# Two-block network in float32 on one core: block 2 heads transposed into other PSUM tiles, VectorE's order set for key rounds and boundary sums, a third relu buffer, the delta solve one step later

## The chip, the cores and the metric

The kernel runs on one core of one Trainium2 chip, as one launch. The metric is the time of that launch on the device in microseconds (us). Of the kernel before, three runs took 2660.15, 2661.12 and 2662.5 us; the median is 2661.12 us.

## The reference

A sequence of 512 tokens of width 1024 goes through two blocks of two layers each. Every layer is a mixer and a feed-forward part (FFN), each with an RMS norm before it, one behind it, and a residual sum. Cut to what matters:

```python
def first_block(x, ...):                      # 2 layers
    h = rms_norm(x, norm_pre_mix[l])
    proj = h @ w_in[l]                        # dilated attention, 8 heads of 64, and
    attn = dilated_attention(aq, ak, av)      # a gated delta rule, 4 heads of 128,
    o = gated_delta_rule(dq, dk, dv, beta, g) # which inverts (I + A) by chunks
    mix = concat([attn, rms_norm(o) * silu(z)]) @ w_out[l]
    x = x + rms_norm(mix, norm_post_mix[l])
    x = x + rms_norm(conv_glu_ffn(rms_norm(x, ...)), norm_post_ffn[l])

def second_block(x, ...):                     # 2 layers
    u_pool, q, k, v, iq, ik, iw = split(rms_norm_2(x, g_pre_mix[l]) @ w_in[l])
    score = einsum('bqh,bqhs->bqs', iw, relu(iq . ik))   # indexer, 8 heads of 64
    keep the 128 best of the allowed keys of each query  # top_k
    b_out = softmax attention of q over the kept keys, 8 heads of 64
    mix = concat([pool_mixer(u_pool), b_out]) @ w_out[l]
    x = x + rms_norm_2(mix, g_post_mix[l])
    x = x + rms_norm_2(square(relu(h @ w_ff1[l])) @ w_ff2[l], g_post_ffn[l])
```

## The kernel before

Everything stays in SBUF but the weights, which stream in. Each product of matrices is done as three matmuls (L234 to L236) of high and low parts, since one pass has not the precision wanted. So each 512 KB piece of weights is loaded by SyncE's (SP's) DMA queue into one of two `wr` buffers (L186), rounded by ScalarE (ACT) into `wh` (L212), and the rest is put into `wl` by VectorE (DVE), for some pieces of block 2 by GpSimd (POOL) (L214).

TensorE's (PE's) results go to PSUM in three sets of banks: `mm` (four, the large products), `ax` (two) and `dx` (two).

The order of the work is that in which the program is written out and a scheduler then lays it down, engine by engine. Each engine works its own row in order. The program is a set of generators: `weave` advances a main one (a product of matrices) and with each of its steps the side ones in `fill` by one step each, so that a `yield` is what moves work between places. Where nothing says otherwise, the scheduler sets an instruction into its engine's row where its own estimate of times makes it ready.

Three places bear on the change.

**Block 2, the indexer** (L1499). For each block `i` of 128 queries, `score(i)` takes eight heads' products with the keys (PE L660, two at a time, in both `ax` banks), lets ACT take the relu of each into an `rl` buffer (L1534; two buffers), copies the first with a weight to `sc` (L1536), and has VectorE add the other seven (L1538). `select(i)` then finds the 128 best keys of `sc` in 16 rounds on VectorE, each a MAX8 (L1551) and a MATCH_REPLACE8 (L1552) over 128(i+1) columns: 256, 384 and 512 for i of 1, 2 and 3. A mask `nm` comes of it (L1555), which the attention reads (L693) and the first block of queries doesn't need. `select(1)` runs beside `score(2)`, `select(2)` beside `score(3)`, and `select(3)` beside the attention. In the same stretch `heads_split` (L663) turns the heads of q and k: four PE transposes (L620) into an `ax` bank, two ACT copies (L667, L761) and a VectorE subtract (L762). Layer 1 of block 2 repeats layer 0 some 614 us later.

**The boundary** (L565), at the end of every mixer and FFN but the last: the sum of squares of the product goes through `rsqrt` on VectorE (L443 to L457, tiny instructions), PE copies the result across partitions (`replicate`, L472), VectorE and ACT update x (L561, L562, L481, L482), and `stats_sum` (L485) adds up the squares of the new x for the next norm, on VectorE and on POOL (L493).

**The delta rule's solve** (`delta_chain`, L964). It gathers small triangles through two scratch tensors in DRAM: SP writes `scx` and `scw` (L1061) and reads them back, spread over 128 partitions, into `dqv` and `dW` (L1062). Four yields later the first PE matmul on `dqv` is written (L1078); `dW` is first read at L1091.

Of the kernel before, what the change touches and what calls it, by code (L numbers as in the profile page):

```python
# [9 lines left out]
F32 = mybir.dt.float32  # L10
# [3 lines left out]
OP = mybir.AluOpType  # L14
AX = mybir.AxisListType

P = 128
S = 512
# [73 lines left out]
class Net:  # L92
# [345 lines left out]
    def rsqrt(self, v, n, out=None, factor=None):  # L438

        V, sm = self.nc.vector, self.sm  # L440
        new = lambda name: sm.tile([P, 16], F32, name=name)[:, :n]
        i = sm.tile([P, 16], I32, name="rqi")[:, :n]
        V.tensor_scalar(i, v.bitcast(I32), 1, None, op0=OP.logical_shift_right)  # L443
        V.tensor_scalar(i, i, -1, RSQ, op0=OP.mult, op1=OP.add)
        y, h, t, u, z = i.bitcast(F32), new("rqh"), new("rqt"), new("rqu"), new("rqz")
        V.tensor_tensor(t, y, y, op=OP.mult)
        V.tensor_scalar(h, v, 64.0 / 9.0, None, op0=OP.mult)
        V.tensor_tensor(t, t, v, op=OP.mult)
        V.tensor_scalar(z, y, -0.375 * RSQ_A, None, op0=OP.mult)
        V.scalar_tensor_tensor(z, t, -RSQ_B, z, op0=OP.add, op1=OP.mult)  # L450
        V.tensor_tensor(t, z, z, op=OP.mult)
        V.tensor_tensor(t, t, h, op=OP.mult)
        V.scalar_tensor_tensor(u, t, -10.0 / 3.0, t, op0=OP.add, op1=OP.mult)
        if factor is not None:
            V.tensor_tensor(z, z, factor, op=OP.mult)
        y = out if out is not None else new("rqy")
        V.scalar_tensor_tensor(y, u, 5.0, z, op0=OP.add, op1=OP.mult)  # L457
        return y

    def col_sums(self, parts, pt):  # L460
# [104 lines left out]
    def boundary(self, B, steps_a, steps_b, lead, gap):  # L565


        gname, l, need_rep, tok = B["nxt"]
        for st in steps_a:
            st()  # L570
            yield
        self.place_next(2, B["pool"], B["wnext"])
        self.prefetch(4)
        for st in steps_b[:lead]:
            st()
            yield
        ra = self.post_rms(B, 0)
        for st in steps_b[lead:lead + gap]:
            st()
            yield  # L580
        rep_a = self.replicate(ra, 2)
        for k in range(NK):
            self.post_update(B, 0, k, rep_a)
        for st in steps_b[lead + gap:]:
            st()
            yield
        rb = self.post_rms(B, 1)
        pts = [self.mm() for _ in range(4)]
        gen = (self.gemm_tok_halves if tok else self.gemm_feat_halves)(pts, self.xs, 8)
        for i in range(2):  # L590
            next(gen)
            yield
        rep_b = self.replicate(rb, 2)
        for k in range(NK):
            self.post_update(B, 1, k, rep_b)
        for n, todo in ((3, lambda: self.stats_sum(0, B["gt"], need_rep)), (5, lambda: self.stats_sum(1, B["gt"], need_rep)),
                        (2, lambda: self.stats_rms(B["gt"])), (2, lambda: None)):
            for i in range(n):
                next(gen)
                yield  # L600
            todo()
        if need_rep:
            self.stats_rep()
        self.first = pts, gen
# [8 lines left out]
        return dict(gt=gt, mixg=[t[:, k] for t in gt for k in range(4)], pool=pool, parts=[])  # L613


    def transposed(self, src):

        pt = self.ax()
        for pr in range(4):
            self.nc.tensor.transpose(pt[:, pr * P:(pr + 1) * P], src[:, pr * P:(pr + 1) * P], self.ident)  # L620
        return pt.rearrange("p (a b) -> p a b", a=4)
# [41 lines left out]
    def heads_split(self, hl, src, t):  # L663


        p, s = self.transposed(src), slice(t * P, (t + 1) * P)
        self.nc.scalar.activation(self.four(src), p, AF.Copy)  # L667
        self.split_out(self.four(src), hl[0][:, :, s], hl[1][:, :, s])

# [294 lines left out]
    def delta_chain(self, pool, D, l, conv):  # L964
# [67 lines left out]
        p = self.dx()  # L1032
# [27 lines left out]
        for src, scr, dst in ((qt, self.scx, X), (qr, self.scw, W)):  # L1060
            nc.sync.dma_start(self.blocks(scr), src)  # L1061
            nc.sync.dma_start(dst.rearrange("p h t c -> p (h t) c"), self.full(scr))  # L1062
        yield
        yield
        yield
        yield

        for lev in (32, 64, 128):
            half, nb = lev // 2, P // lev
# [372 lines left out]
    def mixer2(self, l):  # L1442
        nc, V, T, tc = self.nc, self.nc.vector, self.nc.tensor, self.tc
        with tc.tile_pool(name=f"m2{l}", bufs=1, reuse_waits="tile") as pool:
            wpool = pool.tile([P, 4, P], F32, name="wpool")
            nc.gpsimd.dma_start(wpool, self.a["w_pool_2"][l].rearrange("g c d -> c g d"))
            xs = self.xs
            pts = yield from self.take_first()
            rcol, rrep = self.rcol, self.rrep
            rq = pool.tile([P, NT], F32, name="rq")  # L1450
            V.tensor_scalar(rq, rcol, -0.125, None, op0=OP.mult)
            ri = pool.tile([P, NT], F32, name="ri")
            V.tensor_scalar(ri, rcol, 0.125, None, op0=OP.mult)
            rw = pool.tile([P, NT], F32, name="rw")
            V.tensor_scalar(rw, rcol, 8.0 ** -0.5, None, op0=OP.mult)
            iA = [pool.tile([P, 4, S], F32R, name=n) for n in ("iqT", "ta")]
            hd = self.heads2(pool, pts, ri, lambda x, t: self.heads_split(iA, x, t), 0)
            pt = self.mm()
            yield from self.gemm_small(pt, xs, 72)
            ikw = pool.tile([72, S], F32, name="ikw")  # L1460
            nc.scalar.activation(ikw, pt[:72], AF.Copy)
            nm = [self.c("nchunk")] + [pool.tile([P, (i + 1) * P], F32, name=f"nm{i}") for i in range(1, NT)]
            D, bufs = {}, []
            fill = [hd, self.indexer(pool, D, iA, ikw, rcol, rw, nm)]
            kk = [pool.tile([P, 4, S], F32R, name=n) for n in ("kT", "w3")]
            qq = [pool.tile([P, 4, S], F32R, name=n) for n in ("qT", "w2")]
            v = pool.tile([P, NT, S], F32, name="v")

            def buf(n):
                if not bufs:  # L1470
                    bufs.extend(pool.tile([P, NT, S], F32, name=b) for b in ("qs", "ta"))
                return bufs[n % 2][:, n // 2 % 4]

            self.on_pool.update(range(self.n_get + 2, self.n_get + 14))
            scores = self.split_scores(qq, lambda pr: [t[:, pr] for t in kk])
            att = self.attention(pool, scores, v, lambda i: nm[i], 4, self.dx, 2, buf, lambda: "mix" in D,
                                 lambda i: "scored" in D and D.get("selected", 0) >= i)
            for name in ("k", "q", "v"):
                pts = [self.mm() for _ in range(4)]
                if name == "v":  # L1480
                    fill.append(self.early(att, 6, 1, lambda: "scored" in D))
                yield from self.weave(self.gemm_tok(pts, xs, NK), fill)
                if name == "k":
                    fill.insert(0, self.heads2(pool, pts, rcol, lambda x, t: self.heads_split(kk, x, t), 2))
                elif name == "q":
                    fill.insert(0, self.heads2(pool, pts, rq, lambda x, t: self.heads_split(qq, x, t), 2))
            for t in range(NT):
                nc.scalar.activation(v[:, t, :], pts[t], AF.Copy, scale=rcol[:, t:t + 1])
            mix = self.xs
            fill.append(self.pool_mix(pool, D, rrep, l, wpool, mix))  # L1490
            yield from self.weave(att, fill)
            while fill:
                yield from self.weave(iter([0]), fill)
            yield from self.out_gemm(pool, mix, None, "g_post_mix_2", l, ("iqT", "qT"), ("kT", "v", "w2", "w3", "w4"),
                                     ("qs", "ta"),
                                     lambda n: pool.tile([P, S], F32, name="sc" if n % 2 else "rl", bufs=2),
                                     ("g_pre_ffn_2", l, False, False))

    def indexer(self, pool, D, iA, ikw, rcol, rw, nm):  # L1499
# [25 lines left out]
        def score(i):  # L1525
            w = (i + 1) * P
            sc = pool.tile([P, S], F32, name="sc", bufs=2)
            for h in range(8):
# [1 line left out]
                    ss = [self.ax() for _ in range(2)]  # L1530
                    scores(ss, i, h // 2)
                p = ss[h % 2]
                rl = pool.tile([P, S], F32, name="rl", bufs=2)
                nc.scalar.activation(rl[:, :w], p[:, :w], AF.Relu)  # L1534
                if h == 0:
                    nc.scalar.activation(sc[:, :w], rl[:, :w], AF.Copy, scale=iw[:, i, 0:1])  # L1536
                else:
                    V.scalar_tensor_tensor(sc[:, :w], rl[:, :w], iw[:, i, h:h + 1], sc[:, :w], op0=OP.mult, op1=OP.add)  # L1538
                if h % 2:
                    yield  # L1540
            V.memset(sc[0:64, w - 64:w], -FMAX)
# [4 lines left out]
        def select(i):  # L1546
            w = (i + 1) * P
            sc = scs[i]
            for it in range(16):
                m8 = self.sm.tile([P, 8], F32, name="m8")  # L1550
                V.max(m8, sc[:, :w])  # L1551
                V.match_replace(sc[:, :w], m8, sc[:, :w], MARK)  # L1552
                if (it % 2, 1, it % 4)[i - 1]:
                    yield
# [126 lines left out]
```

## Time and profile before

| | us |
|---|---|
| median of three runs | 2661.12 |
| the profiled execution | 2660.98 |
| span of its trace | 2659.2 |
| PE busy | 2607.6 |
| VectorE busy | 1559.9 |
| ACT busy | 1125.8 |
| POOL busy | 261.3 |

1.8 us of the profiled execution lie outside the trace's span. The share of busy time tells which engine the rest has to keep fed; what a place costs is read from the idle time of that engine in front of an instruction, and from what released it. The clock that PE was granted stands beside it: in a row of a stretch, 1.00 is 2.4 GHz for all of it and 0.50 would be 1.2 GHz for all of it.

### The profile page before, as it was taken

The page shows a single profiled execution, that of the slowest core. Times are in us where ns is not written, and L with a number is a line of the kernel's source. Part 1 is how long each engine was busy: PE and PEld are TensorE (multiplying, and loading weights), DVE is VectorE, ACT ScalarE, POOL GpSimd, SP SyncE. Part 2 cuts the span into 40 slices and gives each one's busy share as a digit, 9 for nine tenths or more (in the row PEclk, how much of TensorE's full clock was granted, in tenths as well). Part 3 has the DMA queues.
Part 4 walks back from the last instruction along what each step waited for, and adds up shares of the span by engine and source line. Part 5 has one row for each costly group of instructions (what it writes and reads, how often), then busy time and mean ns, then how long its engine had stood idle before and what let it go on. Part 6 is the DMA issues. An engine that isn't in the chain of part 4 may idle for free.

```text
span 2659.2 us, 35443 instructions
## 1 busy us (share of the span) xinstructions
PE 2607.6 (98%) x13656; PEld 2111.8 (79%) x13656; DVE 1559.9 (59%) x3122; ACT 1125.8 (42%) x1916; POOL 261.3 (10%) x356
## 2 busy tenths in 40 slices
PE   8999999999999999999999999999999999999998
PEld 7877788888888869888888667888888766988887
DVE  6946676663586576666636875634326785633434
ACT  5346543342443474433424455324224446423322
POOL 2100100000220002000002431000002330100000
PEclk9999999999999999999999999999999999999999
DMA  5321213333324102233332212133333222133232
GB/s 159 94 83 52 80 41 95 96 95 96 95 82 108 48 33 80 87 95 93 95 107 72 72 56 80 49 95 95 95 96 96 63 61 68 57 95 93 90 95 95
DMA packets 155568, 221.83 MB, mean 83 GB/s; under 512 B 25759, under 2 KB 92039, under 8 KB 155399
## 3 DMA queue, kind: packets, MB, share of 16 engines
q1 hardware_dynamic: 154007, 216.92, 27.1%
q0 software_dynamic: 832, 2.63, 0.3%
q8 instruction: 107, 1.75, 0.3%
q14 instruction: 62, 0.51, 0.1%
q10 hardware_dynamic: 560, 0.01, 0.0%
HBM read 212.70 MB, written 6.83 MB: 83 GB/s over the span
## 4 chain that ended last, share of the span: by engine, by line
PE 82%; DVE 13%; ACT 2%; DMA 1%; POOL 1%; issue 1%; SPq 0%; DVEq 0%; ACTq 0%; POOLq 0%
PE mm L234 20%; PE mm L236 20%; PE mm L235 20%; PE dx L236 2%; PE dx L235 2%; PE dx L234 2%; DVE sc L1552 2%; PE ax L236 2%; PE ax L235 2%; PE ax L234 2%; DVE m L1551 2%; PE ax L730 2%; PE mm L711 1%; DVE hl L482 1%; DVE x L562 1%
## 5 line engine op out<-in xcount | busy, mean ns | idle before, releaser
L236 PE MATMUL mm<-hh,wl 128*128 128x512 f32 (+2 forms) x1924 | 738.5, 384 | 0.0
L234 PE MATMUL mm<-hh,wh 128*128 128x512 f32 (+2 forms) x1924 | 737.1, 385 | 1.4 <-ACT wh L212 1.1
L235 PE MATMUL mm<-hl,wh 128*128 128x512 f32 (+2 forms) x1924 | 737.2, 383 | 0.0
L214 DVE TENSOR_TENSOR wl<-wr,wh 128x1024 fp32r<-128x1024 f32 (+1 forms) x312 | 385.6, 1236 | 590.1 <-ACT wh L212 577.1
L212 ACT ACTIVATE wh<-wr 128x1024 fp32r<-128x1024 f32 (+1 forms) x336 | 354.4, 1055 | 729.2 <-PE mm L235 387.2
L234 PEld LDWEIGHTS mm<-hh,wh 128*128 128x128 f32 (+1 forms) x1924 | 362.7, 189 | 78.6 <-ACT wh L212 1.5
L235 PEld LDWEIGHTS mm<-hl,wh 128*128 128x128 f32 (+1 forms) x1924 | 361.9, 188 | 77.4 <-issue 0.7
L236 PEld LDWEIGHTS mm<-hh,wl 128*128 128x128 f32 (+1 forms) x1924 | 361.0, 188 | 74.8
L234 PE MATMUL mm<-wh,hh 128*128 128x512 f32 x524 | 215.8, 412 | 0.0
L235 PE MATMUL mm<-wl,hh 128*128 128x512 f32 x524 | 210.5, 402 | 0.0
L236 PE MATMUL mm<-wh,hl 128*128 128x512 f32 x524 | 209.6, 400 | 0.0
L234 PEld LDWEIGHTS mm<-wh,hh 128*128 128x128 f32 x524 | 99.6, 190 | 28.0 <-issue 3.7
L236 PEld LDWEIGHTS mm<-wh,hl 128*128 128x128 f32 x524 | 99.8, 191 | 23.7
L235 PEld LDWEIGHTS mm<-wl,hh 128*128 128x128 f32 x524 | 100.0, 191 | 22.7 <-issue 1.8
L1265 DVE TENSOR_TENSOR hl<-hq,hh 128x512 fp32r<-128x512 f32 x92 | 63.0, 687 | 73.0 <-ACT hh L1264 72.9
L1378 ACT ACTIVATE fy<-fxc,par 128x512 f32<-128x512 f32 x88 | 67.1, 810 | 78.5 <-DVE fxc L1375 78.5
L1264 ACT ACTIVATE hh<-hq 128x512 fp32r<-128x512 f32 x92 | 57.2, 622 | 94.7 <-PE dx L235 78.8
L481 ACT ACTIVATE hh<-x,par 128x256 fp32r<-128x256 f32 x128 | 60.4, 503 | 78.1 <-DVE x L562 77.8
L1375 DVE TENSOR_TENSOR fxc<-mm,rrep 128x512 f32<-128x512 f32 x88 | 59.9, 688 | 29.8 <-PE mm L236 25.5
L730 PEld LDWEIGHTS ax<-tb,v 128*64 128x64 f32 x640 | 42.8, 136 | 40.0 <-DVE tb L715 11.5
L730 PE MATMUL ax<-tb,v 128*64 128x128 f32 x640 | 68.9, 286 | 4.8 <-DVE tb L715 4.8
L214 POOL TENSOR_TENSOR wl<-wr,wh 128x1024 fp32r<-128x1024 f32 x24 | 57.5, 2394 | 126.8 <-ACT wh L212 126.8
(666 smaller groups left out, 4468.4 us busy)
## 6 DMA issues: line engine op xcount, KB each, us to landing
wr<-in_w_ff_dram SPq DMA_DIRECT2D x128, 512.0 KB, 3.6
wr<-in_w_in_dram SPq DMA_DIRECT2D x96, 512.0 KB, 3.7
wr<-in_ffn_w_in_dram SPq DMA_DIRECT2D x176, 256.0 KB, 3.2
wr<-in_ffn_w_out_dram SPq DMA_DIRECT2D x44, 512.0 KB, 3.5
wr<-in_w_out_dram SPq DMA_DIRECT2D x32, 512.0 KB, 3.6
xt<-in_x_dram SPq DMA_DIRECT2D x4, 512.0 KB, 7.5
scm<-dM SPq DMA_DIRECT2D x2, 1024.0 KB, 4.5
out_dram<-hq SPq DMA_DIRECT2D x8, 256.0 KB, 2.0
```

The source lines that it names most:

```text
L212: nc.scalar.activation(h[:, :n], r[:, :n], AF.Copy)
L214: eng.tensor_tensor(lo[:, :n], r[:, :n], h[:, :n].bitcast(F32), op=OP.subtract)
L234: t.matmul(out, ah, bh, start=first, stop=False, skip_group_check=shared)
L235: t.matmul(out, ah, bl, start=False, stop=False, skip_group_check=shared)
L236: t.matmul(out, al, bh, start=False, stop=last, skip_group_check=shared)
L481: nc.scalar.activation(self.hh[k][:, c], self.x[k][:, c], AF.Copy, scale=g)
L730: T.matmul(o[self.head_rows(e), h // 2 * P:(h // 2 + 1) * P], v[:, j, (h + e) * 64:(h + e + 1) * 64], pT[e][:, j * P:(j + 1) * P], start=j ...
L1264: nc.scalar.activation(h, hid[k], AF.Copy)
L1265: V.tensor_tensor(lo, hid[k], h.bitcast(F32), op=OP.subtract)
L1375: V.tensor_tensor(xc[:, 2:], pt, rrep, op=OP.mult)
L1378: nc.scalar.activation(y, xc[:, 2:], AF.Identity, scale=w(2), bias=self.pcol("ffn_conv_b", l, r))
L1551: V.max(m8, sc[:, :w])
```

## The change

It makes five edits. The squares' first sum at a boundary (VectorE's L493 of the first half) has to stand behind the last instruction of the second half's `rsqrt`. `heads_split` takes a `dx` bank in place of an `ax` bank (96 transposes and their 24 copies in block 2). The delta solve waits five yields in place of four behind its reads. The `rl` buffers are three in place of two. And each MAX8 of a selection has to stand behind the newest add of the scores that has been written out so far. No engine's instructions change in number; POOL's row is the same as before.

```diff
-        V.scalar_tensor_tensor(y, u, 5.0, z, op0=OP.add, op1=OP.mult)
+        self.rsqrt_end = V.scalar_tensor_tensor(y, u, 5.0, z, op0=OP.add, op1=OP.mult).ins
@@ boundary
+        rb_end = self.rsqrt_end
+        def sum_a():
+            with self.tc.issue_after(rb_end):
+                self.stats_sum(0, B["gt"], need_rep)
-        for n, todo in ((3, lambda: self.stats_sum(0, B["gt"], need_rep)), (5, ...
+        for n, todo in ((3, sum_a), (5, lambda: self.stats_sum(1, B["gt"], need_rep)),
@@ heads_split
-        p, s = self.transposed(src), slice(t * P, (t + 1) * P)
+        p, s = self.transposed(src, self.dx()), slice(t * P, (t + 1) * P)
@@ delta_chain
-        yield
-        yield
-        yield
-        yield
+        for _ in range(5):
+            yield
@@ score
-                rl = pool.tile([P, S], F32, name="rl", bufs=2)
+                rl = pool.tile([P, S], F32, name="rl", bufs=3)
-                    V.scalar_tensor_tensor(sc[:, :w], rl[:, :w], iw[:, i, h:h + 1], sc[:, :w], op0=OP.mult, op1=OP.add)
+                    D["added"] = V.scalar_tensor_tensor(sc[:, :w], rl[:, :w], iw[:, i, h:h + 1], sc[:, :w],
+                                                        op0=OP.mult, op1=OP.add).ins
@@ select
-                V.max(m8, sc[:, :w])
+                with self.tc.issue_after(D["added"]):
+                    V.max(m8, sc[:, :w])
```

Line numbers of the changed kernel are 5 to 7 higher behind the boundary: L1538, L1551, L1552 and L762 become L1543, L1558, L1559 and L768; L1061, L1062 and L1078 become L1067, L1068 and L1084.

VectorE's row in block 2, layer 0, where `select(2)` meets `score(3)`: the rounds are MAX and MATCH_REPLACE of 384 columns (m_13312 belongs to the second round, m_13717 to the last), the adds are 128x512. Before, from the fourteenth round on:

```order
L1551 MAX m_13649<-sc 128x8
L1552 MATCH_REPLACE sc<-m_13649,sc 128x384
L1538 SCALAR_TENSOR_TENSOR sc<-rl,iw,sc 128x512
L1551 MAX m_13676<-sc 128x8
L1552 MATCH_REPLACE sc<-m_13676,sc 128x384
L1551 MAX m_13717<-sc 128x8
L1552 MATCH_REPLACE sc<-m_13717,sc 128x384
L1538 SCALAR_TENSOR_TENSOR sc<-rl,iw,sc 128x512
L1555 TENSOR_SCALAR nm_12738<-sc 128x384
```

and now, from the first round on:

```order
L1559 MATCH_REPLACE sc<-m_13282,sc 128x384
L1562 TENSOR_SCALAR nm_12737<-sc 128x256
L1543 SCALAR_TENSOR_TENSOR sc<-rl,iw,sc 128x512
L1558 MAX m_13312<-sc 128x8
L1559 MATCH_REPLACE sc<-m_13312,sc 128x384
L1543 SCALAR_TENSOR_TENSOR sc<-rl,iw,sc 128x512 x2
L1558 MAX m_13361<-sc 128x8
L1559 MATCH_REPLACE sc<-m_13361,sc 128x384
L768 TENSOR_TENSOR w_12743<-qs,qT 128x4x128 x2
L1543 SCALAR_TENSOR_TENSOR sc<-rl,iw,sc 128x512 x2
```

The first add stood behind the fourteenth round and stands behind the first one now; the last two adds now stand ahead of the fifth round, so that twelve of the sixteen rounds of `select(2)` come behind them. Those twelve and the sixteen of `select(3)` are now mixed with the attention's instructions, and `nm_12739`, the mask of the last block, which stood ahead of the last use of `nm_12737`, now stands right in front of its own first use.

VectorE's row at the boundary behind layer 0's mixer of block 1, before:

```order
L448 TENSOR_TENSOR rqt<-rqt,hv 128x2
L493 TENSOR_TENSOR dqk<-dqk,dqq 128x4x256
L450 SCALAR_TENSOR_TENSOR rqz<-rqt,rqz 128x2
L451 TENSOR_TENSOR rqt<-rqz 128x2
L452 TENSOR_TENSOR rqt<-rqt,rqh 128x2
L453 SCALAR_TENSOR_TENSOR rqu<-rqt 128x2
L457 SCALAR_TENSOR_TENSOR rqy<-rqu,rqz 128x2
```

and now:

```order
L448 TENSOR_TENSOR rqt<-rqt,hv 128x2
L450 SCALAR_TENSOR_TENSOR rqz<-rqt,rqz 128x2
L451 TENSOR_TENSOR rqt<-rqz 128x2
L452 TENSOR_TENSOR rqt<-rqt,rqh 128x2
L453 SCALAR_TENSOR_TENSOR rqu<-rqt 128x2
L457 SCALAR_TENSOR_TENSOR rqy<-rqu,rqz 128x2
L493 TENSOR_TENSOR dqk<-dqk,dqq 128x4x256
```

The sum of squares went from the middle of the `rsqrt` to behind it. On PE the four L472 that take `rqy` also stand some nine 256-column matmuls earlier than before.

SP's row in layer 0 of block 1, where the solve's triangles go out and come back, before:

```order
L1061 DMA scx<-vn 128x16x16
L1061 DMA scw<-dS 128x16x16
L186 DMA wr<-in_w_in_dram 128x2x512
L1062 DMA dqv<-scx 128x16x128
L1062 DMA dW<-scw 128x16x128
L186 DMA wr<-in_w_in_dram 128x2x512 x4
```

and now:

```order
L1067 DMA scx<-vn 128x16x16
L1067 DMA scw<-dS 128x16x16
L1068 DMA dqv<-scx 128x16x128
L186 DMA wr<-in_w_in_dram 128x2x512 x2
L1068 DMA dW<-scw 128x16x128
L186 DMA wr<-in_w_in_dram 128x2x512 x3
```

One load of weights that stood ahead of the read of `dqv` stands behind it, and a second one stands between the reads of `dqv` and `dW`. On PE the first L1078 stands four 512-column matmuls and a group of transposes earlier, and the matmuls between it and the first L1091 have grown from nine to nineteen.

## Rows read from the trace of the kernel before

**Rows 1.** The page: busy us by engine, share of the span, instructions.

```profile
PE 2607.6 (98%) x13656; PEld 2111.8 (79%) x13656; DVE 1559.9 (59%) x3122; ACT 1125.8 (42%) x1916; POOL 261.3 (10%) x356
```

**Rows 2.** Waits of PE over the span: waited for, us in total, times, longest.

```profile
PE ax L620 <- ACT rl L1534: 9.4, 4, 4.2
PE dx L1078 <- DMA dqv<-scx: 5.4, 2, 2.9
...
PE ax L472 <- DVE rqy L457: 4.6, 6, 0.9
...
PE ax L472 <- DVE rcol L457: 1.5, 3, 1.0
```

**Rows 3.** Block 2, layer 0, by stretch: length, busy by engine, PEclk, DMA share, GB/s.

```profile
1528.00:1536.00 8.00, 8.00 (x25) 5.75 (x26) 5.77 (x11) 3.29 (x7) 0.00 (x0) 0.57 0.01 2
...
1543.00:1583.00 40.00, 38.58 (x190) 27.00 (x189) 36.27 (x104) 21.35 (x55) 13.39 (x14) 1.00 0.22 67
1583.00:1600.00 17.00, 16.18 (x99) 9.16 (x97) 11.19 (x38) 13.29 (x35) 4.51 (x6) 1.00 0.10 32
```

**Rows 4.** Timeline, block 2, layer 0: start, us, engine line op [idle before <-releaser].

```profile
1509.42 0.54 DVE L1552 MATCH_REPLACE8 sc<-m,sc 128x384 f32<-128x384 f32 x1
...
1512.87 0.56 DVE L1551 MAX8 m<-sc 128x8 f32<-128x384 f32 x1
...
1514.12 0.56 DVE L1551 MAX8 m<-sc 128x8 f32<-128x384 f32 x1
...
1517.50 0.73 ACT L1536 ACTIVATE sc<-rl,iw 128x512 f32<-128x512 f32 x1
...
1522.51 0.39 PE L234 MATMUL mm<-wh,hh 128*128 128x512 f32 x1
1522.74 0.39 PE L235 MATMUL mm<-wl,hh 128*128 128x512 f32 x1
...
1526.51 0.74 DVE L1538 SCALAR_TENSOR_TENSOR sc<-rl,iw,sc 128x512 f32<-128x512 f32 x1
...
1527.35 0.60 ACT L1534 ACTIVATE rl<-ax 128x512 f32<-128x512 f32 x1 [6.24 <-DVE sc L1538]
...
1528.00 0.66 PE L620 MATMUL ax<-cst,qs 128*128 128x128 f32 x4 [4.19 <-ACT rl L1534]
...
1542.43 0.69 DVE L1551 MAX8 m<-sc 128x8 f32<-128x512 f32 x1
...
1543.95 0.69 DVE L1551 MAX8 m<-sc 128x8 f32<-128x512 f32 x1
...
1582.97 0.43 DVE L1555 TENSOR_SCALAR nm<-sc 128x512 f32<-128x512 f32 x1
...
1602.32 0.68 DVE L693 CUSTOM_DVE_ANT_0 qs<-mm,nm 128x512 f32<-128x512 f32 x1
```

**Rows 5.** Timeline of the delta solve, block 1, layer 0: SP's issue, then PE.

```profile
132.18 0.79 SPq L1062 DMA_DIRECT2D dqv<-scx  x1
...
140.82 1.07 PE L1078 MATMUL dx<-dqv,dM 128*128 128x64 f32 x8 [2.93 <-DMA dqv<-scx]
...
144.97 1.00 PE L1091 MATMUL dx<-dY,dW 128*128 128x64 f32 x8
```

**Rows 6.** DMA view of 128 to 145 us: GB/s in 40 slices of 0.425 us.

```profile
GB/s 29 0 0 0 19 120 100 115 109 108 103 140 154 289 395 251 280 318 294 275 279 299 323 280 299 308 279 294 304 299 265 270 188 318 376 313 125 77 77 14
```

**Rows 7.** Timeline of the boundary behind block 1's first mixer: VectorE, POOL, PE.

```profile
345.05 1.22 DVE L493 TENSOR_TENSOR dqk<-dqk,dqq 128x1024 f32<-128x1024 f32 x1
...
346.37 0.16 DVE L451 TENSOR_TENSOR rqt<-rqz 128x2 f32<-128x2 f32 x1
346.56 1.15 DVE L452 TENSOR_TENSOR rqt<-rqt,rqh 128x2 f32<-128x2 f32 x1
...
346.41 2.09 POOL L493 TENSOR_TENSOR dqk<-dqk 128x512 f32<-128x512 f32 x2 [7.16 <-DVE rqz L450]
...
348.66 0.68 PE L472 MATMUL ax<-cst,rqy 128*128 128x128 f32 x4 [0.73 <-DVE rqy L457]
```

More of the change, by code (lines that the diff above doesn't have):

```diff
@@ L595, in boundary @@
             self.post_update(B, 1, k, rep_b)
-        for n, todo in ((3, lambda: self.stats_sum(0, B["gt"], need_rep)), (5, lambda: self.stats_sum(1, B["gt"], need_rep)),
+        def sum_a():
+            with self.tc.issue_after(rb_end):
+                self.stats_sum(0, B["gt"], need_rep)
+        for n, todo in ((3, sum_a), (5, lambda: self.stats_sum(1, B["gt"], need_rep)),
                         (2, lambda: self.stats_rms(B["gt"])), (2, lambda: None)):
@@ L613, in mixg_tiles, with transposed @@
         return dict(gt=gt, mixg=[t[:, k] for t in gt for k in range(4)], pool=pool, parts=[])
-    def transposed(self, src):
-        pt = self.ax()
+    def transposed(self, src, pt=None):
+        pt = self.ax() if pt is None else pt
         for pr in range(4):
@@ L1495, in mixer2 @@
                                      ("qs", "ta"),
-                                     lambda n: pool.tile([P, S], F32, name="sc" if n % 2 else "rl", bufs=2),
+                                     lambda n: (pool.tile([P, S], F32, name="sc", bufs=2) if n % 2 else
+                                                pool.tile([P, S], F32, name="rl", bufs=3)),
                                      ("g_pre_ffn_2", l, False, False))
```

## The prediction

> **What bounds the kernel now.** I read the page first. PE is busy for 2607.6 of 2659.2 us, 98%, VectorE for 59% [rows 1]. So nothing that doesn't shorten a wait of PE, or a stretch of PE at the lower clock, can be worth anything. The change adds and removes no instruction. Then the table of PE's waits: the largest is that of the head transposes L620 for ACT's relu, 9.4 us in four pieces, then the delta solve's wait for `dqv`, 5.4 us in two, and the wait of L472 for the boundary's `rqy`, 4.6 us in six [rows 2]. The edits aim at these three, 19.4 us in all; to them comes what the clock loses behind the first. Last I read the timelines around each.
>
> In block 2 the reader is to see a chain through the row of an in-order engine. VectorE's add L1538 starts at 1526.51, behind a long run of selection rounds; ACT's relu has by then sat 6.24 us idle for the buffer that this add frees, and PE has stood 4.19 us at L620, whose `ax` bank the relu empties [rows 4]. Behind this wait the granted clock is 0.57 over the 8 us from 1528 to 1536 [rows 3]; at the full 2.4 GHz that work would have taken 8.00 x 0.57 = 4.6 us, so 3.4 us are lost beside the wait itself. A layer thus loses 9.4 / 2 + 3.4 = 8.1 us, two layers 16.2 us.
>
> **The change part by part.** The sum is made against the profiled execution's 2660.98 us, of which 1.8 lie outside the span; it stands 0.14 us under the median of the runs, which is nothing here.
>
> *Boundary sums.* Before, VectorE's sum L493 takes 1.22 us in the middle of the second half's `rsqrt`; as it ends it releases POOL's two sums (2.09 us), and beside them the two-column L452 takes 1.15 us where its neighbour L451 takes 0.16 [rows 7]. So `rqy` comes 1.22 + 1.0 = 2.2 us late or a little more, and PE shows 0.73 us of it as a wait at L472 [rows 7]. Now the sum stands behind `rqy`. `rqy` is there 2.2 us sooner; PE stands at L472 nine 256-column matmuls sooner, which is 1.05 us at half the step of a 512-column one, 1522.74 - 1522.51 = 0.23 [rows 4]. 2.2 - 1.05 is still more than the 0.73, so this wait goes: 4.6 us over the six places. The wait of L472 for `rcol` later in the boundary, 1.5 us in three [rows 2], hangs on the same sums, which now follow `rqy`; since all before them comes earlier I count a bit over half of it gained, 0.9. That makes 5.5 us. What VectorE does next, the updates L561 and L562, now runs beside POOL's sums, so some of 2.09 us may fall on VectorE there; they have PE's matmuls of the next product in front of them. If that cover fails, a boundary gives its gain back. Bounds: 2 us (half of the six waits come back), 9 us (the waits of L464 and more of `rcol` go as well).
>
> The Trainium skill, SBUF — State Buffer, section "SBUF: two separate sides", says that a GpSimd operation and a VectorE operation with two SBUF inputs lock each other out of a shared port for a whole instruction. The 1.15 us of L452 agree: 0.16 and about one of POOL's two sums. By that rule an update L562 can be held for one POOL sum, half of 2.09 us, at each boundary, which would take back up to 1.0 us of each; that is the third rival's price, below.
>
> *Delta solve.* The read of `dqv` is issued at 132.18 and PE starts on it at 140.82 after 2.93 us of waiting [rows 5]. From 133.5 us on the queues move about 295 GB/s [rows 6], so this is bandwidth. `dqv` spreads 128 x 2048 floats, 1.05 MB; before it stood one weight load of 0.52 MB and beside it `dW`, another 1.05 MB. Now `dqv` comes first, with weight loads behind it: estimated 1.57 MB at 295 GB/s from about 133.1, which is 138.4, or 139.0 if the loads behind it share more. PE comes to L1078 some 0.9 us sooner (four 512-column steps of 0.23), at 137.0. The wait is then 1.4 to 2.0 in place of 2.93, a gain of 0.9 to 1.5; layer 1, with a wait of 2.5 (5.4 less 2.9), gains 0.4 to 1.2. I take 2.0 for both. Bounds: 0 (all four transfers share the queue evenly, and order buys nothing), 4 (`dqv` lands by 137.5). The read of `dW` falls behind two loads; by the same rate it is down at about 143, and with ten more matmuls in between PE needs it at about 145 as before [rows 5], so that edit is covered by 2 us.
>
> *Block 2: heads, relu buffer, adds ahead of rounds.* The stall itself must go: the add that frees the relu's buffer no longer waits behind thirteen rounds, there is a third buffer, and the transposes don't share `ax`. But the rounds are not gone. They cost 1514.12 - 1512.87 = 1.25 us each at 384 columns and 1543.95 - 1542.43 = 1.52 at 512 [rows 4]. Now every round after the first of `select(2)` stands behind the first add of `score(3)`. That add needs ACT's copy L1536, which in the trace runs from 1517.50 to 1518.2 [rows 4], and PE gets to those scores hardly sooner now. VectorE comes to that place at about 1510, where before its second round ended [rows 4]; so it idles some 7 us in which it used to do rounds. The last adds come when PE is through the scores, before at 1542.4, now 8.1 us sooner, 1534. Then 12 rounds of `select(2)` are left, 12 x 1.25 = 15.0, and `select(3)`, which began at 1542.43 [rows 4], can begin at 1549: VectorE is 6.6 us late.
>
> What it can catch up is its idle time up to the first use of the last mask, at 1602.32 [rows 4]: 40 - 36.27 = 3.7 us in 1543 to 1583 and 17 - 11.19 = 5.8 in 1583 to 1600, together 9.5 us [rows 3]. The mask was ready at 1582.97, so 19 us of slack stand there [rows 4], but slack of the mask isn't free time of VectorE: the attention's own instructions on it (L693, L715) stand between the rounds, and PE waits for each. If all 9.5 us are filled with rounds, the first use comes at 1602.3 + 6.6 - 9.5 = 1599.4, a gain of 2.9 us; if 4.1 are filled, at 1604.8, a loss of 2.5. Walking VectorE's row with these durations I fill about 7.8 and get 1601.1, a gain of 1.2 us per layer, 2.4 in all, with ends of -5 and +5.8. So of the 16.2 us that the stalls and the clock cost, some 14 come back as waits of PE on VectorE inside the attention: at its first blocks (L715 to L730) and in front of the 512-column masks.
>
> **The rivals.**
> A. *VectorE keeps up.* If its idle 7 us don't arise, because PE reaches the scores sooner than I read, or if the attention leaves more gaps than 9.5 us, all 8.1 us per layer stay. For it speaks the slack of 19 us at the mask; against it the 36.27 busy us of 40. Time: 2660.98 - 16.2 - 5.5 - 2.0 = 2637.3.
> B. *Slower: VectorE's queue becomes the bound and brings the clock down.* If it catches up nothing, the first use is 6.6 us late; one wait of PE of the size of 4.19 us then stands in the attention, and such a one was followed by the lower clock for a loss of 3.4 us [rows 3, 4]. That is 10 us lost per layer, with the rest 2660.98 + 20 - 7.5 = 2673.5. It decides the sign once a layer loses over 3.8 us, and shows as slower by over 0.2% from 6.4, that is where less than 3.6 of the 9.5 us are filled. Against it: the 2.93 us wait at `dqv` was not followed by a lower clock, and several shorter waits are likelier than one long. The Trainium skill, TensorE: Matmul & The Clock Gate, section "HAM oscillation — how this bites in real kernels", describes a kernel whose repeated waits of PE bring the clock down each time; by that rule moving one wait into several attention steps is no gain, which is this rival; the trace shows the drop behind 4.19 us and none behind 2.93.
> C. *The boundary's gain doesn't come:* POOL's sums hold up the updates instead, and `rqy` early buys nothing. Then 2660.98 - 2.4 - 2.0 = 2656.6.
>
> **How the numbers follow.** Forecast: 2660.98 - 5.5 - 2.0 - 2.4 = 2651.1, 0.37% faster, chance 0.50; its own range, with the bounds of its three terms taken together but not all at one end, is 2644 to 2660. A has 0.12, C 0.18, B and its milder forms 0.20. A measurement of this kernel can tell about 0.2% from no change, 5.3 us. Faster by more than that: 0.40 of the forecast, all of A, 0.03 of C: 0.55. Slower by more: 0.17 of B. Within: 0.10, 0.15 and 0.03: 0.28. The range of 2637 to 2665 holds the forecast, C, the upper half of A and B's mildest form, about 0.8.
>
> **What would show it.** At 1510 to 1518 VectorE should be idle for about 7 us in front of an add of `score(3)`; PE's wait for relu at L620 and the lower clock at 1528 should be gone; in their place waits of L730 for L715 and one in front of the 512-column products. At the boundaries no wait of L472 for `rqy`, and L452 at 0.16 us. At `dqv` a wait of 1.4 to 2.0 us. The prediction is wrong if PE runs through the attention without those waits (A), if the clock drops in it (B), or if L561 and L562 stretch beside POOL and PE waits there (C).

## The result: 0.54% faster, and the profile after

Ten runs of the changed kernel have a median of 2646.57 us, ten of the kernel before 2660.69; the ratio is 0.9946 with a 95% interval of 0.9932 to 0.9960, so 14 us are gained. The forecast was 2651.1, 0.37% faster, in a range of 2637 to 2665.

The changed kernel's runs are further apart than those of before, 2641.4 to 2654.5 us, and PE's mean granted clock goes with them: 0.998 at the lower end, 0.992 at the upper. By an estimate from these numbers both would be about the same at the full clock, 2641.4 - 0.002 x 2640 = 2636 us and 2654.5 - 0.008 x 2653 = 2633. That spread is part of the explanation below.

PE's waits over the span of the changed kernel, to be read against [rows 2] (waited for: us in total, times, longest):

```profile
PE ax L736 <- DVE tb L721: 7.4, 12, 1.4
PE dx L1082 <- DMA dqv<-scx: 3.9, 2, 2.2
...
PE ax L464 <- DVE gb L493: 1.8, 2, 1.3
...
PE mm L234 <- ACT qs L1431: 1.0, 1, 1.0
```

The wait for relu at L620 and the wait of L472 for `rqy` aren't in the table any more. The wait for `dqv` fell from 5.4 to 3.9 us. The largest is now one inside the attention: L736 (L730 before) for VectorE's copy L721 (L715 before), 4.8 us before and 7.4 now. The wait for ACT's L1431, at the boundary between the blocks, is new. The solve's first matmul, L1078 before, is L1082 in these views (not L1084, as said ahead), and L1091 is L1095.

Block 2, layer 0, by stretch (length, busy by engine, PEclk, DMA share, GB/s), against [rows 3]:

```profile
1503.00:1516.00 13.00, 13.00 (x60) 9.52 (x59) 5.52 (x15) 7.39 (x11) 10.09 (x9) 1.00 0.27 79
...
1576.00:1593.00 17.00, 15.17 (x88) 8.67 (x86) 16.69 (x48) 11.26 (x29) 1.37 (x3) 1.00 0.00 0
1593.00:1607.00 14.00, 13.30 (x55) 8.29 (x55) 8.13 (x24) 9.28 (x21) 0.00 (x0) 0.51 0.11 39
```

VectorE is half idle in the first stretch (5.52 of 13 us) and has no gap left in the second (16.69 of 17). In the third the granted clock is 0.51: nearly all of 14 us at 1.2 GHz, where before the clock was 1.00 from 1543 to 1600. The timeline shows why VectorE idles, when its last mask is ready, and what PE waits for:

```profile
1505.66 0.28 DVE L1562 TENSOR_SCALAR nm<-sc 128x256 f32<-128x256 f32 x1
1512.59 1.07 DVE L1543 SCALAR_TENSOR_TENSOR sc<-rl,iw,sc 128x512 f32<-128x512 f32 x1 [6.65 <-ACT sc L1541]
...
1591.26 0.87 PE L736 MATMUL ax<-tb,v 128*64 128x128 f32 x10 [1.36 <-DVE tb L721]
...
1593.56 0.41 DVE L1562 TENSOR_SCALAR nm<-sc 128x512 f32<-128x512 f32 x1
1593.70 1.54 PE L736 MATMUL ax<-tb,v 128*64 128x128 f32 x10 [0.70 <-DVE tb L721]
...
1594.56 0.68 DVE L699 CUSTOM_DVE_ANT_0 qs<-mm,nm 128x512 f32<-128x512 f32 x1
```

At the boundary of [rows 7], now:

```profile
343.35 0.16 DVE L452 TENSOR_TENSOR rqt<-rqt,rqh 128x2 f32<-128x2 f32 x1
...
343.81 1.22 DVE L493 TENSOR_TENSOR dqk<-dqk,dqq 128x1024 f32<-128x1024 f32 x1
...
344.48 0.60 PE L472 MATMUL ax<-cst,rqy 128*128 128x128 f32 x4
...
345.12 0.75 DVE L561 TENSOR_TENSOR dqk<-dqk,ax 128x256 f32<-128x256 f32 x2
345.18 2.17 POOL L493 TENSOR_TENSOR dqk<-dqk 128x512 f32<-128x512 f32 x2 [8.14 <-PE ax L472]
...
345.79 1.84 DVE L562 TENSOR_TENSOR x<-x,dqk 128x256 f32<-128x256 f32 x2
```

L452 is back at 0.16 us and L472 has no wait in front of it. POOL's sums now meet the updates: two L562 take 1.84 us, where the two L561 of the same size ahead of them, which read one operand from PSUM, take 0.75; PE shows no wait for them here.

Where the 14 us came from is seen by setting PE's instructions of two traces side by side, the n-th of one to the n-th of the other (both have 13656), and taking the difference of their starts at places between the changes, where both rows hold the same instructions. This table is worked out from the traces' PE rows; the columns with a name in italics are kernels of the next section. A minus is a loss.

| gain against before, us | changed | changed, second profile | *bound* | *block2* | *noorder* | *half3* | *early2* |
|---|---|---|---|---|---|---|---|
| delta solve, two layers | 1.5 | 0.9 | -0.5 | -4.5 | 0.8 | 0.9 | 1.3 |
| seven boundaries | 7.4 | 7.4 | 1.5 | -2.2 | 7.1 | 7.3 | 7.2 |
| block 2, layer 0 | 0.3 | 5.1 | 0.1 | 4.3 | 4.7 | 9.6 | 10.5 |
| block 2, layer 1 | 4.5 | 4.8 | 0.4 | 4.7 | 5.0 | 10.0 | 10.9 |

One execution stands behind each column, and each holds the falls of the clock that this execution had: *bound* had falls at boundaries, and *block2* at the solves and at boundaries, that the changed kernel's profiles hadn't, which is why their columns don't show what their medians do. Up to 1.9 us more (*bound*) lie ahead of the first solve. Of the changed kernel's seven boundaries one loses: the one between the blocks, 0.6 us.

The order rule does one thing that the description of the change doesn't name: PE's own row in the attention is laid out otherwise too, at 75 places of each layer (the score matmuls L666, for one, stand in other groups around L736). *order_only* has the same 75, *noorder* none.

### The profile page after: what moved, and what is told of

Same layout as the page of the kernel before. It is cut to its first block, busy times and chain, and to the rows that moved or that the text cites. A ratio compares the mean times of both kernels' runs of the same rounds, so it can differ in the third digit from the quotient of the medians.

```text
span 2645.2 us, 35427 instructions
## 1 busy us (share of the span) xinstructions
PE 2605.6 (99%) x13656; PEld 2113.5 (80%) x13656; DVE 1549.0 (59%) x3122; ACT 1126.3 (43%) x1916; POOL 264.9 (10%) x356
## 5 line engine op out<-in xcount | busy, mean ns | idle before, releaser
L736 PE MATMUL ax<-tb,v 128*64 128x128 f32 x640 | 71.2, 293 | 7.8 <-DVE tb L721 7.4
L736 PEld LDWEIGHTS ax<-tb,v 128*64 128x64 f32 x640 | 44.4, 139 | 42.0 <-DVE tb L721 16.8
```

The source lines that it names most:

```text
L736: T.matmul(o[self.head_rows(e), h // 2 * P:(h // 2 + 1) * P], v[:, j, (h + e) * 64:(h + e + 1) * 64], pT[e][:, j * P:(j + 1) * P], start=j ...
```

## The experiments

**The parts alone.** The kernel before with one part of the change each: *bound* has the boundary edit, *delta* the fifth yield, *block2* the three edits of block 2.

```diff
# bound: the first half's sum behind rsqrt's last instruction
+            with self.tc.issue_after(rb_end):
+                self.stats_sum(0, B["gt"], need_rep)
# delta
-        (four) yield
+        for _ in range(5):
+            yield
# block2: dx in heads_split, rl bufs=3, V.max under issue_after(D["added"])
```

> The kernel before with the boundary edit alone. Theory (the edits act each in its own place and their gains add): the waits of L472 for rqy go, and by the gains that the changed kernel shows at its seven boundaries (1.4, 0.1, 1.4, -0.6, 1.5, 1.8, 1.5 us) it is 7 us faster than before, ratio about 0.9974; block 2 still has its 4.2 us wait and the lower clock behind it. Rival (the gain of the change is all in block 2, a boundary's early rqy is lost again within the boundary): within 2 us of before.

> The kernel before with the fifth yield alone. Theory: the wait for dqv falls by about 1.9 us in layer 0 and by less in layer 1, 3 us in all, ratio about 0.9988. Rival (the read of dqv is bound by bytes that the other transfers take in any order, and dW or the weights come late instead): within 1 us of before.

> The kernel before with the three edits of block 2 (dx banks, third rl buffer, rounds behind the newest add) and neither boundary nor delta edit. Theory: the 9.4 us of waits at L620 and the lower clock behind them go, waits of L730 for L715 grow by some 2.5 us, and the time depends on whether the clock falls in the attention: 2647 to 2648 us where it doesn't, 2655 to 2657 where it does for 13.7 us in one layer and 3.4 in the other; so single runs spread over 8 us or more. Rival (VectorE keeps up and the spread of the changed kernel comes from the delta or boundary edits): single runs within 2 us of each other.

Measured against 25 runs of before with a median of 2662.84 us (gains are worked out from the ratios): *bound* 2654.49 us, ratio 0.9971 (0.9960 to 0.9982), a gain of 7.7 us: the theory. *delta* 2660.39, 0.9998 (0.9988 to 1.0007), 0.5 us: the rival's number, not told from no change, with an interval that just reaches the theory's 3 us. The rival's mechanism isn't seen: the profile shows the wait for `dqv` down from 5.4 to 3.9 us, as in the changed kernel. Side by side with before its first layer gains 1.8 us and its second loses 2.0, with the clock at 1.2 GHz for 6.8 us from 840.5, behind a wait of 2.21 us. *block2* 2660.23, 0.9992 (0.9981 to 1.0004), twelve runs from 2654.0 us at a mean clock of 0.996 to 2672.6 at 0.988. So block 2's edits by themselves gain little on the median, 2.1 us, and spread the time over 19 us, further up than I expected. Its one profile gains 4.3 + 4.7 us in the two layers and loses 6.7 at solves and boundaries, which it doesn't touch and where the clock fell; what the slow end at 2672.6 us lost, and where, no profile shows. The three gains add up to 7.7 + 0.5 + 2.1 = 10 of the 14 us; the 4 us between are inside what the intervals leave open.

**Which edit takes the stall away.** *order_only* has the rule for the rounds alone; *dxrl* has the `dx` banks and three `rl` buffers without the rule.

> The kernel before with one block 2 edit alone: every round behind the newest add; heads still in ax banks, two rl buffers. Theory (the stall at L620 comes from the add that stands behind fourteen rounds): the 4.2 us wait is gone or under 1 us, and so is the lower clock behind it. Rival (the stall comes from sharing ax or from two rl buffers): a wait of 4 us stays.

> The kernel before with dx banks and three rl buffers, without the order rule; the first add of score(3) still stands behind fourteen rounds. Theory: PE passes L620, but stands at the scores L660 a little later, since both ax banks and all rl buffers wait for the same add at 1526: a wait of 2 to 4 us moves there, PE's waits in block 2 fall by less than half. Rival (banks and buffers are the cause): no wait over 1 us in 1515 to 1545.

Each is one execution. *order_only*: no wait of PE at L620 from 1500 to 1550, so the rule alone removes the stall; the theory. But it took 2673.48 us. Its stretches:

```profile
1604.00:1624.00 20.00, 19.76 (x80) 12.45 (x81) 10.23 (x29) 12.68 (x29) 0.00 (x0) 0.50 0.08 27
2222.00:2242.00 20.00, 19.79 (x80) 12.48 (x81) 10.23 (x29) 12.68 (x29) 0.00 (x0) 0.50 0.07 27
```

In both layers 20 us of the attention ran at 1.2 GHz, behind the same waits for L715's copies that the changed kernel has (7.4 us, 12 times, 1.4 the longest). Side by side with before its layers lose 3.9 and 3.4 us. It lies 12.5 us behind before's profiled execution; 5.3 of them were lost at the two delta solves, which it doesn't touch, with 10.2 us of lower clock there. *dxrl* took 2653.85 us; PE's wait moved to the scores:

```profile
1532.84 0.50 PE L660 MATMUL ax<-ikT,iqT 64*128 64x512 f32 x1 [1.51 <-ACT rl L1535]
```

That is the theory's kind, but shorter than its 2 to 4 us: over two layers 9.4 us of waits became 3.0. No lower clock came behind it in either layer (in *noorder*, below, which has a like wait of 1.57 us, 3.4 us of it came in one of the two). Side by side with before its layers gain 4.7 and 5.1 us, as much as all three edits of block 2 together gain in *block2*. The stall has two cures, then: the rule takes it away and makes VectorE late, banks and buffers shrink it to 1.5 us and leave VectorE early.

**Is it VectorE's load in the attention?** *half3* is the changed kernel with half of `select(3)`'s rounds.

```diff
-            for it in range(16):
+            for it in range(8 if i == 3 else 16):
```

> The changed kernel with 8 of the 16 rounds of select(3) left out, so the mask of the last 128 queries is not the reference's; VectorE has 8 x 1.52 = 12.2 us less to do beside each attention. Theory (VectorE's load there makes the waits of L736 and the falls of the clock): waits of L736 for L721 fall from 7.4 to under 3 us, no lower clock between 1545 and 1615 and the same stretch of layer 1, median 2636 us or a little less, spread smaller than 13 us. Rival (the clock falls there for the short matmuls of the attention, whatever VectorE does): the lower clock stays in some runs, median 2643 us or more.

Measured 2633.67 us, 0.9891 (0.9877 to 0.9906), runs from 2631.7 to 2636.5 at a clock of 0.997 to 0.999. The waits, and the two stretches:

```profile
PE ax L736 <- DVE tb L721: 2.9, 6, 1.0
```

```profile
1576.00:1593.00 17.00, 17.00 (x112) 9.96 (x110) 13.06 (x38) 14.82 (x37) 1.81 (x3) 1.00 0.11 31
1593.00:1607.00 14.00, 13.74 (x117) 9.52 (x117) 7.25 (x20) 13.43 (x28) 0.00 (x0) 1.00 0.01 2
```

PE is busy for all of the 17 us in which it had gaps of 1.8 us, and the clock doesn't fall, here or in layer 1's attention. The theory holds in this profile: with 12 us less on VectorE beside the attention, the waits shrink to 2.9 us and no lower clock follows them. Two things stay open. The other three runs have no profile, and two of the four had a mean clock of 0.997 where the profiled one had 0.999. And with the rounds some yields went too, so PE's row in the attention differs from the changed kernel's too, at 60 places of each layer; that the load on VectorE alone did it isn't shown.

**The same kernel again, and the change without its rule.**

```diff
# noorder: the changed kernel, but
-                with self.tc.issue_after(D["added"]):
-                    V.max(m8, sc[:, :w])
+                V.max(m8, sc[:, :w])
```

> The changed kernel once more, with a profile of another execution. Theory (where the clock falls varies from run to run, the waits don't): the same waits of PE within 0.3 us each, the lower clock in other places or for other lengths than the 3.4, 13.7 and 3.4 us of the first profile, median 2646 us within 3. Rival (the clock falls at fixed places of this kernel): the same three places with the same lengths.

> The changed kernel without the order rule on the selection's rounds; boundary, delta, dx banks and third rl buffer stay. Theory (the rule makes VectorE late and so brings the clock down in the attention, and the dx banks with three buffers already take the stall from 4.2 to 1.5 us): clock 0.997 or more in most runs, median 2642 to 2645 us, faster than the changed kernel's 2646.6 by 2 to 4 us, and its runs closer together. Rival (the rule is what pays): median 2650 us or more, the lower clock behind 1530.

The second profile of the changed kernel has the same two waits in layer 0's attention, and no lower clock behind them:

```profile
1591.98 0.87 PE L736 MATMUL ax<-tb,v 128*64 128x128 f32 x10 [1.36 <-DVE tb L721]
...
1594.42 0.87 PE L736 MATMUL ax<-tb,v 128*64 128x128 f32 x10 [0.70 <-DVE tb L721]
```

and for the stretch, as above:

```profile
1593.00:1607.00 14.00, 13.01 (x91) 8.12 (x91) 10.68 (x32) 12.06 (x29) 0.00 (x0) 1.00 0.14 39
```

1.36 and 0.70 us in both profiles, 0.51 in one and 1.00 in the other behind them. The theory holds in that the clock's falls vary by execution while these waits don't (the totals differ by more than the 0.3 us I expected: L736 7.4 and 6.7, `dqv` 3.9 and 4.4); the 3.4 us at the second delta solve were there both times, and the third place, layer 1's attention, again for 3.4 us, so places repeat more than I had said. Layer 0's gain is 0.3 us in one profile and 5.1 in the other; that fall cost 4.8 us. Five runs gave 2642.48 us, 0.9935 (0.9922 to 0.9949).

*noorder* took 2646.49 us, 0.9942 (0.9929 to 0.9955): the same as the changed kernel, above the 2642 to 2645 I expected and below the rival's 2650. Within the whole change the rule gives as much as it takes.

How often the clock fell in the attention is read from all the profiles, two layers each. With the rule as it stands (both profiles of the changed kernel, *block2*, *order_only*) it fell in seven of eight layers, for 3.4, 13.7 or 20.5 us, each time behind the wait of 1.36 us. Without the rule (before, *bound*, *delta*, *dxrl*, *noorder*) it fell in one of ten, in *delta*, whose attention is the old one:

```profile
1590.22 0.65 PE L730 MATMUL ax<-tb,v 128*64 128x128 f32 x6 [0.83 <-DVE tb L715]
```

```profile
1591.40:1594.80 3.40, 3.40 (x10) 1.24 (x9) 1.50 (x7) 2.52 (x7) 0.00 (x0) 0.50 0.43 154
```

In *half3* it fell in none of two. So the rule brings the falls, though the old attention isn't free of them. Whether it does so through VectorE's lateness alone or also through PE's changed row, no run parts.

**A version that fills the gap.** If VectorE is late because it idles 6.65 us in front of the first add of `score(3)`, rounds of `select(2)` belong there. *early* does six ahead of the first scores in place of one; *early4* is the same with four yields in the delta solve; *early2* also does four rounds of `select(1)` first in place of two.

```diff
# early
-                if (it % 2, 1, it % 4)[i - 1]:
+                if (it % 2, it >= 5, it % 4)[i - 1]:
# early2
+                if (it % 2 and it > 1, it >= 5, it % 4)[i - 1]:
```

> The changed kernel, but select(2) does six rounds ahead of the first scores of score(3) in place of one. Theory (VectorE's 6.65 us of idle time at 1506 to 1512 us is what it lacks in the attention, and the dense attention is where PE waits and the clock falls): the idle time is filled with five rounds of 1.25 us, VectorE is 6 us less behind in the attention, the waits of L736 for L721 fall from 7.4 us to the 4.8 of before or less, the lower clock in the attention is rarer, median 2640 us or a little under, single runs closer together than 13 us. Rival (the clock falls in the attention whatever VectorE's lateness is): same median as the changed kernel within 2 us, same spread. Second rival (the five rounds hold up the first add of score(3), since scores come while rounds run): slower by some 1 us per layer.

> The kernel with six rounds first (as in the run with select(2)'s early rounds), but the delta solve with four yields as before. Theory (the fifth yield is worth 1.5 us of waits for dqv, less than the clock's spread): within 3 us of 2636.4, a little slower if anything. Rival (the fifth yield costs more than it saves because the clock falls at the delta solve): 2 to 5 us faster, 2632 to 2634.

> The kernel with six rounds of select(2) first, and in addition four rounds of select(1) ahead of the first scores of score(2) in place of two. Theory (VectorE idles 2.26 us in front of the first add of score(2), which two rounds of 0.98 us fill, and each microsecond it is less late takes waits out of the attention): waits of PE on VectorE in the attention fall by 1 to 2 us a layer, median 2632 to 2635 us. Rival (the steps that are moved bring score(3) earlier against the heads of k and q and open a new wait): 2637 us or more.

*early* took 2636.36 us, 0.9907 (0.9893 to 0.9922); *early4* 2638.27, 0.9901 (0.9885 to 0.9918); *early2* 2634.71, 0.9898 (0.9884 to 0.9911). All are clear of the interval of the changed kernel's ten runs (0.9932 and up); that of its five later runs (0.9922 and up) *early* just touches. The two stretches of *early2*, and its waits:

```profile
1503.00:1516.00 13.00, 13.00 (x62) 9.08 (x60) 12.55 (x25) 7.06 (x12) 9.45 (x8) 1.00 0.25 67
...
1576.00:1593.00 17.00, 16.59 (x110) 9.99 (x109) 13.77 (x44) 14.38 (x37) 1.43 (x3) 1.00 0.08 31
```

```profile
PE ax L736 <- DVE tb L721: 4.5, 8, 0.8
```

VectorE is busy for 12.55 of the 13 us in which it had 5.52, and 13.77 of 17 later, where it had 16.69. Against the changed kernel the waits for L721 fell from 7.4 to 4.5 us, with no longer one than 0.8, and its profile has no lower clock in the attention of either layer. In the table above it gains 10.5 and 10.9 us in block 2's layers, 5 to 6 more than the changed kernel in its second profile. *early4* tells nothing on the fifth yield: 1.9 us apart, with overlapping intervals; its rival's 2632 to 2634 us didn't come. The two rounds of `select(1)` gain 1.7 us on the median, also within the intervals; the median is the theory's, but the waits that *early2* was to take out of the attention fell little against *early*: 2.9 us for L721 and 2.5 for the scores (below) became 4.5 and none.

*early*'s theory was right on the idle time (0.52 us are left in front of that add) and the median was better than its 2640 us; its spread wasn't: 2632.2 to 2645.8 us, 13.6 us, at clocks of 0.998 and 0.992. Its waits for L721 fell to 2.9 us, but a new one came, in front of the scores:

```profile
PE mm L666 <- DVE amin L699: 2.5, 4, 0.9
```

Behind it the clock fell again in the attention, for 3.4 us in *early*'s layer 0 and for 3.4 and 10.2 us in *early4*'s two layers. Other falls stand at the delta solves and at boundaries. Side by side with before, the attention takes back 1.7 and 0.3 us of what the scores gained in *early*, where it took 9.6 and 5.8 in the changed kernel's first profile and 4.7 and 5.5 in its second. So *early* gains mostly by shorter waits; that the falls became rarer, as its theory had it, these profiles don't show.

## Why the prediction was right, step by step

**The reading of the stall** held: the add behind the rounds, the relu buffer, the bank. With the rule the waits at L620 are gone from the trace (*order_only*), and the lower clock that stood behind them, [rows 3], with them. Its price was right as well: from the heads' transposes to the end of the scores the changed kernel gains 8.4 and 8.8 us in the two layers, side by side with before, against 8.1.

**Boundary sums**, forecast 5.5 us: measured 7.7 in *bound* and 7.4 in the table, a third more than the term and inside its 2 to 9. I had counted the wait for `rqy` and part of `rcol`'s; that `rcol`'s nearly went (1.5 to 0.3 us) and the wait of L464 for `dqq` shrank (1.4 to 1.0) I had only in the bound, and that L472's wait for `r` (0.7 us) went and L464's for `qT` shrank (1.1 to 0.6) not at all. With the two new waits named below taken off, some 2 us of the gain stand in none of these. The third rival's mechanism is there, two L562 at 1.84 us beside POOL's sums, about 1.1 us over their usual time; it stays on VectorE, since PE has the next product to do there. The Trainium skill, SBUF — State Buffer, section "SBUF: two separate sides", which makes a VectorE operation with two SBUF inputs wait for a whole GpSimd operation, fits: one of POOL's two sums is half of 2.17 us. Behind block 1's FFNs it wasn't free: the wait of L464 for `gb` grew from 0.6 us in one place to 1.8 in two, and at the second of them, the boundary between the blocks, PE also waits 1.0 us for ACT's L1431, whose four copies all stand behind L516 now (two of them stood ahead of it). That boundary loses 0.6 us.

**Delta solve**, forecast 2.0 us: the first layer's wait went from 2.93 to 1.66 us and PE started on `dqv` at 138.73, inside the 138.4 to 139.0 worked out from the bytes:

```profile
138.73 1.97 PE L1082 MATMUL dx<-dqv,dM 128*128 128x64 f32 x16 [1.66 <-DMA dqv<-scx]
146.17 1.08 PE L1095 MATMUL dx<-dY,dW 128*128 128x64 f32 x8
```

The second layer's went only from 2.5 to 2.2, and in both profiles the clock fell behind it, for 3.4 us from 842.2. So the table's 1.5 and 0.9 us are 1.9 and 1.6 won in the first layer and 0.4 and 0.6 lost in the second, where 0.4 to 1.2 were forecast; by time alone the edit can't be told from none. `dW` was in time: there is no wait at L1095 (0.3 us in *half3* and *noorder*). Its cover was thinner than the 2 us named: by the same estimate the 3.1 MB up to the end of `dW` take until 143.8, not 143.

**Block 2**, forecast 1.2 us a layer: the two profiles give 0.3 and 4.5, and 5.1 and 4.8; *block2*'s runs 2.1 for both layers, with an interval that holds 2.4. That 2.1 lies near 2.4 is partly luck: in *block2*'s profile the layers gain 9.0 us and falls at solves and boundaries take most of it back. By the profiles the term was mis-sized, 4.8, 9.9 and 9.0 us for both layers against 2.4, two of them over its upper end of 5.8. Right were the idle time (6.65 us against 7), its cause (ACT's copy L1541), the last add (the memset behind it starts at 1529.3, which with the 4.2 us that PE was ahead by then is 1533.5 in the old time, against 1534), the twelve rounds left, and that a large part of the stall's price comes back in the attention (9.6 and 5.8 us in the first profile, 4.7 and 5.5 in the second, where some 14 for both layers were forecast). Two steps were off. VectorE caught up more than I filled in: the first use of the last mask came at 1594.56, 7.8 us before the old 1602.32 and so 3.6 us of block 2's own, over the 2.9 I had as the most. More idle time was not the reason. From the last add to that use, before and now:

```profile
1542.40:1602.30 59.90, 57.65 (x307) 38.05 (x306) 49.59 (x144) 36.95 (x95) 17.90 (x20) 1.00 0.18 55
```

```profile
1529.30:1594.50 65.20, 60.69 (x316) 39.89 (x315) 60.86 (x181) 38.50 (x97) 18.17 (x20) 0.99 0.14 41
```

VectorE's idle time went from 10.3 to 4.3 us, so 6.0 us were filled, less than my 7.8; but its busy time grew by 11.3 us only, not by the 15.0 that I had for twelve rounds. Which of its instructions make up the difference isn't worked out here. And a part of the price is paid in clock, which I had left wholly to rival B, behind one wait of 4 us: it fell behind a wait of 1.36 us, with one of 0.70 in the fall, in one profile's layer 0 for 13.7 us (14 x 0.49 x 2), in the other's not at all.

**The rivals.** A (VectorE keeps up) came in part, as far as the second profile's 5 of 8.1 us a layer. B's mechanism came, at smaller waits than I gave it and at a smaller price than its 10 us a layer: in *order_only* both layers lose 3.4 to 3.9 us against before (by the same setting side by side), about the 3.8 at which B was to decide the sign. That its 2673.48 us are B's 2673.5 is chance, since 5.3 us of it were lost at the delta solves. What I had against B, that no lower clock followed the 2.93 us wait at `dqv`, held for that trace only: in the changed kernel it followed waits of 2.20 and 2.45 us there. In the changed kernel's profiles the attention's falls were shorter than in *order_only*, 13.7, 3.4 and 3.4 us, and one layer had none. The Trainium skill, TensorE: Matmul & The Clock Gate, section "HAM oscillation — how this bites in real kernels", which the prediction set beside B, fits as far as repeated waits of PE bring the clock down; its waits are for DMA and 3 to 5 us long, and those here brought it down at 1.36 us and less. C did not come, though at the boundaries behind block 1's FFNs a part of the gain was lost again, as said above.

The sum then: 5.5 + 2.0 + 2.4 = 9.9 us forecast, 7.4 + 1.5 + 4.8 + 0.3 ahead of the first layer = 14.0 in the profile. The direction was right, and so was each part's mechanism as far as said above; of the terms, the delta solve's was too large and the other two too small.

## What to carry to other kernels

Moving an in-order engine's small, urgent instruction ahead of long work removes the stall, but look what the engine does while it waits for that instruction's input: here 6.65 us of idle time on VectorE came back as waits and lower clock 80 us later, and five rounds put into that gap took another 7 to 10 us off (by the ratios to before, against the changed kernel's five later runs and its first ten). Where a kernel keeps PE 98% busy, short waits close together can cost more by the clock than by themselves, and not in every run; so look at the mean granted clock of the runs before believing a difference of a few microseconds. Price each part of such a change by itself: here the plainest, one add behind an `rsqrt`, gave over half of the gain.

## What the runs showed of the hardware that I had not expected

PE's clock fell to 1.2 GHz behind a wait of 1.36 us between short matmuls in one execution and not in the next of the same kernel, with the same waits; the stretches lasted from 3.4 us to 20 us, and the longest (*order_only*, twice) were in the attention. Still shorter waits were followed by it, at a boundary of *block2* one of 0.54 us:

```profile
2299.94 0.35 PE L464 MATMUL ax<-ones,qT 128*128 128x1 f32 x2 [0.54 <-DVE qT L493]
```

```profile
2301.20:2304.60 3.40, 3.40 (x18) 3.40 (x18) 3.09 (x16) 0.68 (x2) 0.00 (x0) 0.50 0.39 102
```

Nor was the kernel with the longest wait in block 2 the least steady: the kernel before, whose wait of 4.19 us was followed by the lower clock in both layers of its profile, had ten runs within 4.4 us and all 51 of its runs within 7.9 us (2658.58 to 2666.46), against 13 us in ten runs of the changed kernel and 19 us in twelve of *block2*, whose waits there are shorter.
